# One output projection for both units of the sample, and layer 1's gates, transform and outputs in natural token order

## The chip, the core and the metric

The kernel runs on one core of a Trainium2 chip. The metric is the time of one execution in microseconds on the device. The kernel before took 1991.91 us (median of three runs: 1982.99, 1991.91, 1994.77).

## What is computed

A trunk of two layers is applied with the same weights to two groups of tokens: a prompt of 512 and a sample of 1024, 1024 channels wide, in float32. The change touches the second layer, called layer 1 in the code. Cut to what matters:

```python
def odd_layer(x, c, pre_g, post_g, ada_w, ada_b, w_in, w_out, rpb, lin):
    shift, scale, gate = adaln(c, ada_w, ada_b)
    h = rmsnorm(x, pre_g) * (1 + scale[:, None, :]) + shift[:, None, :]
    p = jnp.einsum('bsd,de->bse', h, w_in)
    qc, kc, vc, gc, ud, gd = split_cols(p, CD_SPLITS)      # 768, 768, 768, 768, 256, 256 columns
    oc = neighbourhood_attention(heads(qc), heads(kc), heads(vc), rpb).reshape(b, s, C_WIDTH)
    od = fourier_mixing(ud, lin)                           # real part of a 2-D DFT, then a linear map
    mixed = jnp.concatenate([oc * jax.nn.silu(gc), od * jax.nn.silu(gd)], axis=-1)
    y = rmsnorm(jnp.einsum('bse,ed->bsd', mixed, w_out), post_g)
    return x + gate[:, None, :] * y
```

The attention looks at a grid 64 tokens wide; a query sees a window of 8 rows by 16 columns.

## The kernel before

Tokens are worked on in units of 512: the sample's units 0 and 1, and the prompt as unit 2. Every matrix product is made of three products of rounded parts (high by high, high by low, low by high), so each operand exists twice, as `hh` and `hl`, and each weight as `who` and `wlo`: a weight block of 256 KB is loaded into a staging buffer `wso` (four of them), ScalarE casts the high part, and VectorE or GpSimd subtracts it to get the low part (`load_w`, L350). The pairs of high and low parts lie in rings: four pairs of tag `w`, and in layer 1 two more of tag `wx` (`w_pair`, L342).

Layer 1's attention works on blocks of queries, 8 grid rows by 16 columns. So its results are written in that order: within 512 tokens first the column block i, then the row r, then the column j. Before, all that meets the attention's result is in that order too: the gates (`chan_gemm` with `blocks`, L381, reads its tokens rearranged for q, g and d), the transform's result (by the order of the rows of its table, L79), and the rows of the residual input and of the outputs, which `blocks_of` (L267) picks out of DRAM as 8 groups of 16 rows.

The output projection `s3` (L845) is called for units 2, 0 and 1 in turn. For a unit it takes the operand, which `s3_operand` (L826) makes of eight pairs of loads, attention result `m` and gate `g` (name `og`): one multiply on GpSimd or VectorE, a cast on ScalarE and a subtraction on VectorE for each. Then come the gate row (`gate_row`, L254, 512 KB, one buffer), and four weight jobs of 256 columns: four weight blocks, two products groups of 48 matmuls each (`tok_gemm`, L366; two tiles of 128 tokens share one PSUM buffer, of which there are three), the squares on ScalarE (L863) and the product with the gate row on VectorE (L864). When a unit is through, the four residual rows `xo` of 512 KB are loaded into the three buffers of tag `sp`, in which the operand's loads lie too, the sum is made (L886) and the output row goes out. The next unit's operand is loaded under the former one's sums. So each unit loads all of `w_out_cd`, 4 MB, for itself.

All loads and stores are issued from SP's one queue in program order, and an issue that has to wait holds those behind it. A scheduler sets the order on each engine when the program is built.

## Time and profile before

| | us |
|---|---|
| three runs: lowest, median, highest | 1982.99, 1991.91, 1994.77 |
| profiled execution, its own time | 1982.05 |
| its span, first to last instruction | 1980.3 |
| TensorE busy in the span | 1895.3 (96%) |
| VectorE, ScalarE, GpSimd busy | 1219.5, 933.1, 636.3 |
| mean granted TensorE clock | 0.983 |

Busy times are of one profiled execution. In rows of the trace PE is TensorE, DVE VectorE, ACT ScalarE, POOL GpSimd and SPq the queue from which transfers are issued. L142 is line 142 of the kernel, out<-in are the program's names without buffer numbers, xN counts equal instructions, and a bracket at a row's end is the idle time before it and what ended that.

### The profile page before, as it was taken

The numbers are of one execution on the slowest core, as the hardware profiler recorded it, in microseconds if no ns is written. First come the engines' busy times: TensorE is split into PE (matmuls) and PEld (weight loads), VectorE is DVE, ScalarE is ACT, GpSimd is POOL, SyncE is SP. The second block draws the span as 40 slices with busy tenths as digits, with TensorE's granted clock in tenths as the row PEclk, the third lists the DMA queues.
The fourth block names the chain that finished last, engine by engine and source line by source line (L and its number), as shares of the span: only waits on it lengthen the run. The fifth ranks groups of instructions, "written<-read, shape, count | busy, mean of one in ns | idle before, by whom it ended". The sixth has DMA issues, their size and how long they took to land.

```text
span 1980.3 us, 38139 instructions
## 1 busy us (share of the span) xinstructions
PE 1895.3 (96%) x13720; PEld 1634.3 (83%) x13720; DVE 1219.5 (62%) x3139; ACT 933.1 (47%) x2211; POOL 636.3 (32%) x566
## 2 busy tenths in 40 slices
PE   6999999999999999999999999999999999998896
PEld 3889778999889888888876678888878888877895
DVE  3788765255768666767755686563766526667452
ACT  3466544343366544565544454454544424445331
POOL 2822334254622211121111222444323313344231
PEclk8999999999999999999999999999999999999998
DMA  9755555467764323344454775564777646687573
GB/s 339 226 175 170 165 177 176 143 204 226 249 222 129 110 76 95 99 143 132 134 159 153 225 231 172 190 205 141 231 215 230 188 141 191 191 245 232 183 228 105
DMA packets 270797, 358.75 MB, mean 181 GB/s; under 512 B 26648, under 2 KB 177528, under 8 KB 270608
## 3 DMA queue, kind: packets, MB, share of 16 engines
q1 hardware_dynamic: 270608, 356.32, 57.3%
q8 instruction: 108, 1.77, 0.4%
q14 instruction: 81, 0.66, 0.1%
HBM read 268.08 MB, written 88.16 MB: 180 GB/s over the span
## 4 chain that ended last, share of the span: by engine, by line
PE 77%; DMA 11%; DVE 6%; issue 2%; POOL 2%; ACT 1%; SPq 1%; ACTq 0%; DVEq 0%; POOLq 0%
PE y L142 7%; PE c1g L142 5%; PE c1q L142 5%; PE c1k L142 5%; PE t1v L142 5%; PE tvb L142 4%; PE gga L142 3%; PE ggb L142 3%; PE sas L142 3%; PE oas L142 3%; PE ptas L146 3%; PE tqa L142 2%; PE tqb L142 2%; DMA wso<-w_out_cd 2%; PE ocs L636 2%; PE sbs L772 2%
## 5 line engine op out<-in xcount | busy, mean ns | idle before, releaser
L142 PE MATMUL y<-who,hhm 128*128 128x256 f32 x768 | 220.6, 289 | 9.7 <-ACT hhm L841 4.9
L142 PE MATMUL y<-wlo,hhm 128*128 128x256 f32 x768 | 219.6, 288 | 7.5 <-POOL wlo L361 7.0
L142 PE MATMUL y<-who,hlm 128*128 128x256 f32 x768 | 218.8, 288 | 4.4 <-DVE hlm L842 4.3
L142 PEld LDWEIGHTS y<-who,hhm 128*128 128x128 f32 x768 | 147.9, 193 | 13.7 <-ACT hhm L841 5.6
L142 PEld LDWEIGHTS y<-wlo,hhm 128*128 128x128 f32 x768 | 147.9, 193 | 9.0 <-POOL wlo L361 7.4
L142 PEld LDWEIGHTS y<-who,hlm 128*128 128x128 f32 x768 | 148.4, 194 | 7.7 <-DVE hlm L842 5.3
L683 ACT ACTIVATE eas<-sas,nmas 128x512 f32<-128x512 f32 x128 | 86.8, 683 | 71.0 <-DVE nmas L679 70.9
L361 POOL TENSOR_TENSOR wlo<-wso,who 128x512 fp32r<-128x512 f32 x48 | 66.1, 1378 | 128.5 <-ACT who L360 119.2
L993 POOL TENSOR_TENSOR bics<-TTcs,mkc 128x288 f32<-128x288 f32 (+1 forms) x72 | 65.4, 910 | 127.7 <-DVE mcs L1006 106.5
L620 DVE TENSOR_TENSOR ptlas<-ptas,pthas 128x512 fp32r<-128x512 f32 x128 | 85.6, 684 | 18.6 <-ACT pthas L618 18.3
L674 DVE TENSOR_REDUCE mxas<-sas 128x1 f32<-128x512 f32 x128 | 86.4, 683 | 11.5 <-PE sas L142 10.7
L360 ACT CAST who<-wso 128x512 fp32r<-128x512 f32 x96 | 58.5, 616 | 63.3 <-DMA wso<-w_out_cd 22.6
L864 DVE TENSOR_TENSOR y<-y,rowg 128x256 f32<-128x256 f32 x96 | 39.9, 420 | 77.5 <-ACT ysq L863 66.7
L618 ACT CAST pthas<-ptas 128x512 fp32r<-128x512 f32 x128 | 70.3, 591 | 32.4 <-PE ptas L146 26.8
L142 PE MATMUL t1v<-wh1v,hl 128*128 128x256 f32 x288 | 82.5, 287 | 0.0
L142 PE MATMUL t1v<-wh1v,hh 128*128 128x256 f32 x288 | 82.0, 285 | 0.0
L142 PE MATMUL t1v<-wl1v,hh 128*128 128x256 f32 x288 | 81.6, 283 | 0.0
L1011 ACT ACTIVATE ecs<-ecs,ngmcs 128x288 f32<-128x288 f32 (+1 forms) x96 | 54.7, 571 | 54.6 <-DVE ngmcs L1009 53.2
L146 PE MATMUL ptas<-ident,eas 128*128 128x128 f32 x512 | 77.1, 272 | 1.5 <-DVE ptlas L620 1.5
L142 PE MATMUL oas<-ptlas,Vas 128*128 128x256 f32 x256 | 69.4, 297 | 1.1 <-DVE ptlas L620 1.1
L142 PE MATMUL oas<-pthas,Vas 128*128 128x256 f32 x256 | 69.1, 285 | 0.0
L863 ACT ACTIVATE ysq<-y 128x256 f32<-128x256 f32 x96 | 36.6, 382 | 67.9 <-PE y L142 49.9
(614 smaller groups left out, 6471.8 us busy)
## 6 DMA issues: line engine op xcount, KB each, us to landing
aw<-ada_w SPq DMA_DIRECT2D x48, 512.0 KB
wso<-w_out_ab SPq DMA_DIRECT2D x48, 256.0 KB
wso<-w_out_cd SPq DMA_DIRECT2D x48, 256.0 KB
kcs<-k1s SPq DMA_DIRECT2D x24, 384.0 KB
kbs<-k0s SPq DMA_DIRECT2D x16, 512.0 KB
ws1k<-w_in_cd SPq DMA_DIRECT2D x28, 256.0 KB
wskb<-w_in_ab SPq DMA_DIRECT2D x24, 256.0 KB
wsqb<-w_in_ab SPq DMA_DIRECT2D x24, 256.0 KB
```

What stands on the lines that cost most here:

```text
L142: self.nc.tensor.matmul(out, l, r, start=start, stop=stop, skip_group_check=True)
L146: self.nc.tensor.transpose(out, in_, self.ident[:k, :k])
L360: nc.scalar.copy(hi, st)
L361: (nc.vector if c in dve else nc.gpsimd).tensor_sub(lo, st, hi)
L618: nc.scalar.copy(h[:rows, :w], pt[:rows, :w])
L620: nc.vector.tensor_sub(lo[:rows, :w], pt[:rows, :w], h[:rows, :w])
L636: self.nc.tensor.matmul(out[x:x + HD], v, p, start=n < 2, stop=False, tile_position=(0, x), skip_group_check=True)
L674: nc.vector.tensor_reduce(mx[:, c:c + 1], ps, op=ALU.max, axis=AX.X, negate=True)
L683: nc.scalar.activation(e[:, 512 * c:512 * c + 512], pss[c], AF.Exp, bias=nmx, accum_out=den[:, c:c + 1])
L864: nc.vector.tensor_mul(ys[j][:, c], ps[:, t], G[:, c])
L993: nc.gpsimd.tensor_add(b, T[:, :, wo:wo + w], self.mcol[:, kind, wo:wo + w].unsqueeze(1).to_broadcast([P, nrow, w]))
L1011: nc.scalar.activation(e, e, AF.Exp, bias=ngm, scale=0.125, accum_out=den)
```

## The change

The sample's two units share their weights: a new `s3_two` takes the weight jobs in two halves, jobs 0 and 1 for unit 0 and then for unit 1, then jobs 2 and 3 for unit 0 and unit 1. The prompt still has an `s3` of its own, ahead of them. The gate row of the sample is loaded once, into the attention's one key buffer (tag `k`). In that stage weight pairs rotate through a ring of twelve (`self.wend`): four `w`, two `wx`, and buffers that the attention no longer needs (two of tag `q`, two of `pt`, two pairs out of `V`). Unit 0's sums lie in buffers of tag `e`, unit 1's in those of tag `x`.

Only the queries and the attention's result keep the block order. Gates, transform and the rows of residual and output are in the tokens' natural order; `s3_operand` reads the attention's result (k below 6) rearranged when it multiplies it by the gate, and writes the product over the gate.

```diff
@@ -75,8 +75,7 @@
         H, Q = S // 2, S // 4
         ang = lambda t, k: 2 * np.pi * ((t[:, None] * k[None, :]) % S) / S
         norm = 0.5 / np.sqrt(S * 64.0)
-
-        b = np.arange(S).reshape(S // 512, 8, 4, 16).transpose(0, 2, 1, 3).reshape(-1)
+        b = np.arange(S)
         t, quarter = np.arange(Q), np.array([Q])
         rows = []
         for k in (b[0::2], b[1::2]):
@@ -129,7 +128,7 @@
         self.gs, self.gp = self.G
         self.unit_of = [(self.gs, 0), (self.gs, 1), (self.gp, 0)]
 
-        self.wn, self.np, self.wx, self.rope_of = 0, 0, None, None
+        self.wn, self.np, self.wx, self.wend, self.rope_of = 0, 0, None, None, None
         self.pre, self.early, self.idle = {}, {}, True
 
 
@@ -251,8 +250,8 @@
             nc.vector.scalar_tensor_tensor(mod, mod, 1.0, self.adb[:, l, 2, ks].unsqueeze(2).to_broadcast([P, 4, 2]),
                                            op0=ALU.add, op1=ALU.mult)
 
-    def gate_row(self, l, g, nm):
-        t = self.sb.tile([P, D], F32, tag="row", name="row" + nm, bufs=RB)
+    def gate_row(self, l, g, nm, tag="row", bufs=RB):
+        t = self.sb.tile([P, D], F32, tag=tag, name="row" + nm, bufs=bufs)
         self.dma(t, self.modd[l][g.idx:g.idx + 1, :].to_broadcast([P, D]))
         return t
 
@@ -263,11 +262,6 @@
             src = self.a["x_sample" if g.idx else "x_prompt"][0][512 * (i // 4):512 * (i // 4) + 512]
             return src.rearrange("(a r) d -> r a d", r=4)[i % 4]
         return self.x1[g.name, i // 4][(i % 4) * P:(i % 4) * P + P, :]
-
-    def blocks_of(self, full, g, i):
-
-        v = full.rearrange("(h r i j) d -> h i r j d", r=8, i=4, j=16)
-        return v[i // 4, i % 4]
 
     def operand(self, nm, c):
         return (self.sb.tile([P, 2, 512], F32R, tag="hh", name=f"hh{nm}{c}", bufs=HB),
@@ -341,11 +335,14 @@
 
     def w_pair(self, shape, name):
         self.wn += 1
-        if self.wx and self.wn % (WB + WX) >= WB:
-            pool, tag, bufs = self.wx, "wx", WX
+        if self.wend:
+            tags, bufs = self.wend[self.wn % len(self.wend)]
+            pool = self.wx if tags[0][:2] == "wx" else self.sb
+        elif self.wx and self.wn % (WB + WX) >= WB:
+            pool, tags, bufs = self.wx, ("wxh", "wxl"), WX
         else:
-            pool, tag, bufs = self.sb, "w", WB
-        return [pool.tile(shape, F32R, tag=tag + x, name=f"w{x}{name}", bufs=bufs) for x in "hl"]
+            pool, tags, bufs = self.sb, ("wh", "wl"), WB
+        return [pool.tile(shape, F32R, tag=t, name=f"w{x}{name}", bufs=bufs) for x, t in zip("hl", tags)]
 
     def load_w(self, src, name, dve=()):
 
@@ -836,59 +833,103 @@
             st = pool.tile([P, 2, 512], F32, tag="sp", name=f"og{l}{u}{k}", bufs=SPB)
             self.dma(st[:, 0], self.md[l, n, k][:, us])
             self.dma(st[:, 1], self.gd[l, n, gu, k])
-            t = st[:, 0]
-            (nc.vector if k % 2 else nc.gpsimd).tensor_mul(t, t, st[:, 1])
+            t, m = st[:, 1], st[:, 0]
+            tv, mv = t, m
+            if l == 1 and k < 6:
+
+                tv, mv = t.rearrange("p (r i j) -> p r i j", r=8, i=4), m.rearrange("p (i r j) -> p r i j", r=8, i=4)
+            (nc.vector if k % 2 else nc.gpsimd).tensor_mul(tv, mv, tv)
             nc.scalar.copy(hh, t)
             nc.vector.tensor_sub(hl, t, hh)
         return [[o[i] for o in ops] for i in range(2)]
 
-    def s3(self, l, u, tag="x", H=None, step=None, last=None):
+    def s3_tiles(self, l, u, tag):
+
+        pool = self.sb
+        return ([pool.tile([P, D], F32, tag=tag, name=f"y{l}{u}{j}", bufs=XB if tag == "x" else EB) for j in range(4)],
+                [pool.tile([P, 4], F32, tag="yss", name=f"yss{l}{u}{j}", bufs=8) for j in range(4)])
+
+    def s3_w(self, l, u, job):
+        return self.load_w(self.a["w_out_ab" if l == 0 else "w_out_cd"][0][:, 256 * job:256 * job + 256], f"o{l}{u}{job}", W3)
+
+    def s3_job(self, l, u, H, G, w, job, ys, ss, after=None):
+
+        nc, pool = self.nc, self.sb
+        c = slice(256 * job, 256 * job + 256)
+        for jp in range(2):
+            ps = self.pD(f"y{l}{u}{job}{jp}").rearrange("p (t c) -> p t c", t=2)
+            self.tok_gemm(ps, H, w, jp)
+            for t in range(2):
+                j = 2 * jp + t
+                sq = pool.tile([P, 512], F32, tag="scr", name=f"ysq{l}{u}{job}{j}", bufs=SCB)
+                nc.scalar.activation(sq[:, 0:256], ps[:, t], AF.Square, accum_out=ss[j][:, job:job + 1])
+                nc.vector.tensor_mul(ys[j][:, c], ps[:, t], G[:, c])
+            if after:
+                after(jp)
+
+    def s3_x(self, l, u, j, tag):
+        g, gu = self.unit_of[u]
+        x = self.sb.tile([P, D], F32, tag=tag, name=f"xo{l}{u}{j}", bufs=SPB if tag == "sp" else XB)
+        self.dma(x, self.x_src(l, g, 4 * gu + j))
+        return x
+
+    def s3_end(self, l, u, jp, ys, ss, xs):
 
         nc, pool = self.nc, self.sb
         g, gu = self.unit_of[u]
         n = g.name
+        rs = []
+        for j in (2 * jp, 2 * jp + 1):
+            nm = f"{l}{u}{j}"
+            s1 = pool.tile([P, 1], F32, tag="ys1", name="ys1" + nm, bufs=2)
+            nc.vector.tensor_reduce(s1, ss[j], op=ALU.add, axis=AX.X)
+            rs.append(self.rsqrt(pool, s1, 1.0 / D, 1, "yr" + nm))
+        for t, x in enumerate(xs):
+            j = 2 * jp + t
+            y = ys[j]
+            nc.vector.scalar_tensor_tensor(y, y, rs[t], x, op0=ALU.mult, op1=ALU.add)
+            if l == 0:
+                self.dma(self.x1[n, gu].rearrange("(a r) d -> r a d", r=4)[j], y)
+            else:
+                i = 4 * gu + j
+                self.dma(self.o["y_sample" if g.idx else "y_prompt"][0][i * P:(i + 1) * P, :], y)
+
+    def s3(self, l, u, tag="x", H=None, step=None, last=None):
+
+        g = self.unit_of[u][0]
         H = H or self.s3_operand(l, u)
         G = self.gate_row(l, g, f"g{l}{u}")
-        ys = [pool.tile([P, D], F32, tag=tag, name=f"y{l}{u}{j}", bufs=XB if tag == "x" else EB) for j in range(4)]
-        ss = [pool.tile([P, 4], F32, tag="yss", name=f"yss{l}{u}{j}", bufs=4) for j in range(4)]
+        ys, ss = self.s3_tiles(l, u, tag)
         for job in range(4):
-            c = slice(256 * job, 256 * job + 256)
-            w = self.load_w(self.a["w_out_ab" if l == 0 else "w_out_cd"][0][:, c], f"o{l}{u}{job}", W3)
-            for jp in range(2):
-                ps = self.pD(f"y{l}{u}{job}{jp}").rearrange("p (t c) -> p t c", t=2)
-                self.tok_gemm(ps, H, w, jp)
-                for t in range(2):
-                    j = 2 * jp + t
-                    sq = pool.tile([P, 512], F32, tag="scr", name=f"ysq{l}{u}{job}{j}", bufs=SCB)
-                    nc.scalar.activation(sq[:, 0:256], ps[:, t], AF.Square, accum_out=ss[j][:, job:job + 1])
-                    nc.vector.tensor_mul(ys[j][:, c], ps[:, t], G[:, c])
+            self.s3_job(l, u, H, G, self.s3_w(l, u, job), job, ys, ss)
             if step:
                 step()
         r = last and last()
...
+        xt = "sp" if (l, u) in XSP else "x"
+        for jp in range(2):
+            self.s3_end(l, u, jp, ys, ss, [self.s3_x(l, u, j, xt) for j in (2 * jp, 2 * jp + 1)])
         return ys, r
+
+    def s3_two(self, l, H):
+
+        G = self.gate_row(l, self.gs, f"g{l}s", "k", KB)
+        Hs, Y = [H, None], [self.s3_tiles(l, 0, "e"), None]
+        for half in range(2):
+            ws = {}
+            for u in range(2):
+                if u == 1 and half == 0:
+                    Hs[1], Y[1] = self.s3_operand(l, 1), self.s3_tiles(l, 1, "x")
+                xs = {}
+                for job in (2 * half, 2 * half + 1):
+                    if u == 0:
+                        ws[job] = self.s3_w(l, 0, job)
+                    if job == 3:
+                        xs = {jp: [self.s3_x(l, u, j, "sp") for j in (2 * jp, 2 * jp + 1)] for jp in range(1)}
+
+                    def after(jp):
+                        x = xs.get(jp) or [self.s3_x(l, u, j, "sp") for j in (2 * jp, 2 * jp + 1)]
+                        self.s3_end(l, u, jp, *Y[u], x)
+                    self.s3_job(l, u, Hs[u], G, ws[job], job, *Y[u], after if job == 3 else None)
 
 
     def scratch1(self):
@@ -930,7 +971,7 @@
             return
         for c in range(2):
             ps = self.pD(f"c{nm}{c}")
-            self.chan_gemm(ps, H, w, c, typ in "qgd")
+            self.chan_gemm(ps, H, w, c, typ == "q")
             if typ == "q":
                 self.spill_hl(ps, self.qd[1, n, 2 * q + c], gu, 1.0, f"{nm}{c}")
             elif typ == "k":
@@ -1249,9 +1290,10 @@
                     if kind == "v2":
                         for q in range(3):
                             self.attn_c(gs, 1, q)
-            H = ops[0]
-            for u in (2, 0, 1):
-                _, H = self.s3(1, u, H=H, last=(lambda: self.s3_operand(1, (u + 1) % 3)) if u != 1 else None)
+            _, H = self.s3(1, 2, H=ops[0], last=lambda: self.s3_operand(1, 0))
+            self.wend = ([(("wh", "wl"), WB)] * WB + [(("wxh", "wxl"), WX)] * WX + [(("qh", "ql"), QB)] * QB +
+                         [(("pth", "ptl"), PTB)] * PTB + [(("V", "V"), VB)] * (VB // 2))
+            self.s3_two(1, H)
 
 
 @with_exitstack
```

The scheduler moves instructions in three places. The first is SP's queue where the sample's projection begins; `wso` is a weight block, `og` an operand's two halves (`m1s`, `g1s`), `rowg` the gate row, `y_prompt` an output row. Before:

```order
L139 DMA y_prompt<-y_23440 8x16x1024
L139 DMA wso_24357<-w_out_cd 128x2x256
L139 DMA og_24627<-m1s_126 128x512
L139 DMA og_24627<-g1s_118 128x512
L139 DMA rowg_24079<-mod_235 128x1024
L139 DMA wso_24363<-w_out_cd 128x2x256
L139 DMA y_prompt<-y_23441 8x16x1024
L139 DMA og_24633<-m1s_127 128x512
L139 DMA og_24633<-g1s_119 128x512
L139 DMA y_prompt<-y_23442 8x16x1024
L139 DMA og_24641<-m1s_128 128x512
L139 DMA og_24641<-g1s_120 128x512
```

and with the change:

```order
L138 DMA y_prompt<-y_23440 128x1024
L138 DMA og_24359<-m1s_126 128x512
L138 DMA og_24359<-g1s_118 128x512
L138 DMA wso_24787<-w_out_cd 128x2x256
L138 DMA wso_24793<-w_out_cd 128x2x256
L138 DMA y_prompt<-y_23441 128x1024
L138 DMA og_24365<-m1s_127 128x512
L138 DMA og_24365<-g1s_119 128x512
L138 DMA y_prompt<-y_23442 128x1024
L138 DMA og_24373<-m1s_128 128x512
L138 DMA og_24373<-g1s_120 128x512
L138 DMA og_24379<-m1s_129 128x512
```

Before, the operand of unit 1 begins there with the gate row, a weight and the prompt's outputs among its loads, and further weights behind; with the change its loads stand together behind the second prompt output, with the last two weights of the fourth job and two outputs among them.

The second place is ahead of it in the same queue, where the attention's last heads still run (`Vcs` are their values, `wso_23861` a weight of the prompt's last job). With the change:

```order
L138 DMA Vcs_22607<-v1s_196 128x1x384
L138 DMA og_24027<-m1s_132 128x512
L138 DMA Vcs_22609<-v1s_196 96x1x384
L138 DMA og_24027<-g1s_116 128x512
L138 DMA rowg1s<-mod_235 128x1024
L138 DMA og_24033<-m1s_133 128x512
L138 DMA wso_23861<-w_out_cd 128x2x256
L138 DMA og_24033<-g1s_117 128x512
```

The gate row of the sample (`rowg1s`) is new there; before, the operand's load `og_24033` followed `og_24027` at once.

The third is ScalarE's order at the attention's last two heads (`ofcs`, `ptccs` and `ecs` are the attention's; `who` a weight's cast, `ysq` a square of the projection's sums). Before:

```order
L630 COPY ptccs_22746<-ptcs_22742 96x384
L1011 ACTIVATE ecs_22795,dencs_22803<-ecs_22795,ngmcs_22801 128x288
L645 COPY ofcs_22708<-ocs_22619 64x512
L630 COPY ptccs_22790<-ptcs_22786 128x384
L863 ACTIVATE ysq_23788,yss_23443<-y_23739 128x256
L863 ACTIVATE ysq_23791,yss_23444<-y_23739 128x256
```

and with the change:

```order
L627 COPY ptccs_22746<-ptcs_22742 96x384
L1052 ACTIVATE ecs_22795,dencs_22803<-ecs_22795,ngmcs_22801 128x288
L357 CAST who_24097<-wso_24095 128x512
L642 COPY ofcs_22708<-ocs_22619 64x512
L627 COPY ptccs_22790<-ptcs_22786 128x384
L865 ACTIVATE ysq_23788,yss_23443<-y_23739 128x256
L357 CAST who_24103<-wso_24101 128x512
L865 ACTIVATE ysq_23791,yss_23444<-y_23739 128x256
```

Casts of the sample's first weights (`who_24097`, `who_24103`) have moved ahead of the attention's copy and of the square.

## Rows read from the trace of the kernel before

**Rows 1.** Windows by stage: length, busy time of each engine, clock, DMA share, GB/s.
```profile
core 0: us, PE busy (x) PEld busy (x) DVE busy (x) ACT busy (x) POOL busy (x), PEclk, DMA share, GB/s
1700.00:1760.00 60.00, 60.00 (x369) 48.31 (x369) 36.97 (x116) 24.96 (x62) 19.65 (x21) 1.00 0.64 199
1856.50:1963.20 106.70, 94.87 (x768) 94.06 (x766) 49.24 (x83) 34.26 (x99) 30.41 (x26) 0.95 0.59 193
1963.20:1980.30 17.10, 0.21 (x2) 0.01 (x1) 3.67 (x8) 0.95 (x4) 1.10 (x2) 0.64 0.44 147
```

**Rows 2.** Timeline of TensorE, 1856.5 to 1963.2 us: the products after a stop.
```profile
1875.39 0.58 PE L142 MATMUL y<-wlo,hhm 128*128 128x256 f32 x1 [6.06 <-POOL wlo L361]
...
1930.21 0.51 PE L142 MATMUL y<-who,hhm 128*128 128x256 f32 x1 [3.28 <-DVE y L864]
...
1940.60 0.38 PE L142 MATMUL y<-who,hhm 128*128 128x256 f32 x1 [1.52 <-ACT who L360]
...
1941.94 0.39 PE L142 MATMUL y<-wlo,hhm 128*128 128x256 f32 x1 [0.96 <-POOL wlo L361]
```

**Rows 3.** Windows behind the long stop and in the stage's undisturbed end.
```profile
1875.40:1877.40 2.00, 2.00 (x9) 2.00 (x10) 1.99 (x4) 1.61 (x7) 1.61 (x1) 0.50 0.86 295
...
1946.00:1963.20 17.20, 17.20 (x147) 17.20 (x146) 6.06 (x13) 4.08 (x14) 2.39 (x3) 1.00 0.03 7
```

**Rows 4.** Timeline of VectorE: products with the gate row that waited for it.
```profile
1874.02 0.42 DVE L864 TENSOR_TENSOR y<-y,rowg 128x256 f32<-128x256 f32 x1 [4.93 <-DMA rowg<-mod]
...
1928.70 0.42 DVE L864 TENSOR_TENSOR y<-y,rowg 128x256 f32<-128x256 f32 x1 [5.75 <-DMA rowg<-mod]
```

**Rows 5.** Groups of instructions, 1856.5 to 1963.2 us: casts of weights.
```profile
L360 ACT CAST who<-wso 128x512 fp32r<-128x512 f32 x27 | 16.4, 616 | 23.7 <-DMA wso<-w_out_cd 22.6 <-PE y L142 0.8
```

**Rows 6.** Tile og: issues and low parts, unit 1 in layer 1, then layer 0.
```profile
L139 SPq DMA_DIRECT2D og<-m1s x8: 319/339/793, 1861.2 to 1892.9; - x8
...
L842 DVE TENSOR_TENSOR hlm<-og,hhm x8: 680/694/1777, 1874.8 to 1899.2; 128x512 fp32r<-128x512 f32 x8
...
L139 SPq DMA_DIRECT2D og<-m0p x8: 319/380/467, 317.3 to 338.5; - x8
...
L842 DVE TENSOR_TENSOR hlm<-og,hhm x8: 684/693/1781, 324.7 to 345.7; 128x512 fp32r<-128x512 f32 x8
```

**Rows 7.** The end: chain of waits (one row), then timeline of VectorE.
```profile
1961.67 10.07 DMA xo<-x_s
...
1965.39 1.28 DVE L886 SCALAR_TENSOR_TENSOR y<-y,yr112r,xo 128x1024 f32<-128x1024 f32 x1
...
1971.84 1.28 DVE L886 SCALAR_TENSOR_TENSOR y<-y,yr113r,xo 128x1024 f32<-128x1024 f32 x1 [5.11 <-DMA xo<-x_s]
```

**Rows 8.** Windows: loads near the start, and residual and output rows alone.
```profile
20.00:40.00 20.00, 16.35 (x106) 9.79 (x104) 6.76 (x7) 5.93 (x10) 8.32 (x6) 0.94 1.03 360
...
1968.00:1973.00 5.00, 0.00 (x0) 0.00 (x0) 1.16 (x1) 0.00 (x0) 0.00 (x0) 0.50 0.51 207
```

**Rows 9.** Windows of the key products (first) and of the query products alone.
```profile
1266.00:1700.00 434.00, 71.50 (x288) 52.74 (x288) 8.25 (x12) 6.93 (x12) 1.00 0.62 191
...
1266.00:1700.00 434.00, 72.91 (x288) 53.02 (x288) 8.25 (x12) 7.04 (x12) 1.00 0.62 191
```

**Rows 10.** Timelines of TensorE, SP and ScalarE at the last heads; a page group.
```profile
1813.76 0.30 PE L142 MATMUL scs<-kcs,qlcs 128*128 128x288 f32 x1
...
1815.36 0.76 SPq L139 DMA_DIRECT2D og<-g1s  x1
...
1828.05 2.95 SPq L139 DMA_DIRECT2D wso<-w_out_cd  x2
...
1834.97 0.58 ACT L645 COPY ofcs<-ocs 64x512 f32<-64x512 f32 x1 [1.35 <-PE ocs L636]
...
L993 POOL TENSOR_TENSOR bics<-TTcs,mkc 128x288 f32<-128x288 f32 (+1 forms) x72 | 65.4, 910 | 127.7 <-DVE mcs L1006 106.5
```

23 lines of the change are left out of this document (removed).

## Prediction

> **What bounds the kernel now.** I read the windows by stage first. While layer 1's gates are projected TensorE is busy for 60.00 of 60 us; from the sample's first output product to its last (1856.5 to 1963.2 us, 768 products) it is busy for 94.87 of 106.70; behind the last product 17.10 us pass in which it does nothing [rows 1]. So the early part is bound by TensorE, and the last 124 us are where a change of loads and order can pay. Next I looked for TensorE's stops in that stage: four, 6.06, 3.28, 1.52 and 0.96 us, 11.8 together, which is all that is missing from the busy time [rows 2]. Then the clock: undisturbed it starts 147 products in 17.2 us at a granted 1.00, one every 0.117 us; just after the long stop 9 in 2 us at 0.50, 1.2 GHz, one every 0.21 [rows 3]. 768 products at 0.117 are 89.9 us, so 106.7 - 89.9 = 16.8 us is the most this stage can give: 11.8 of stops, 5.0 of restarts at the low clock.
>
> What ends the stops? VectorE's product with the gate row waits 4.93 and 5.75 us for the row's load, at 1874.02 and 1928.70 [rows 4]; it is what empties the three PSUM buffers, and TensorE starts again at 1875.39 and 1930.21. There is one buffer for that row, and its load can only be issued when the former unit is through with it. The last two stops name ScalarE's cast and GpSimd's low part of a weight [rows 2]; of the casts, 27 in the stage, 22.6 us of idle time before them ends with a weight's landing [rows 5]. The second unit loads the same 4 MB again.
>
> **What the change takes and adds, stage by stage.**
>
> *The sample's projection.* Sixteen weight loads of 256 KB, 16 casts of 0.62 us and 16 low parts go. The gate row is loaded once, into the attention's key buffer, some 45 us before it is used, so neither wait of [rows 4] is left. Twelve pairs of buffers (four ordinary, two of layer 1, six of the attention) let three of the four weight jobs be made while the prompt's sums still run. All four stops lose their cause. What is late next is unit 1's operand: it was needed after four jobs of unit 0, now after two. Two jobs are 192 products, 22.5 us, so it is wanted at 1856.5 + 22.5 = 1879. Its first load stands behind the second prompt output in SP's queue, as before (1861.2), so I start it at 1860. Bounds for its length: in layer 0, with fewer weights between its loads, a stream of eight took from the first issue at 317.3 to the end of the last low part at 346.4 (345.7 and a median 0.69), 29.1 us; in this stage it took from 1861.2 to 1899.9, 38.7 us, with nine weight loads, the gate row and two prompt outputs among its loads [rows 6]. Now two weight loads and two outputs stand among them (the SP rows in the section on the change), so I take the 29: done at 1889. TensorE's new order spends the wait on the other pair of token tiles; behind its last wait 45 products of the first job are left, 5.3 us. So that job ends at 1894.3 instead of 1879 + 96 x 0.117 = 1890.2: 4 us late. Between nothing and 13.7 (1899.9 - 1.2 + 5.3 - 1890.2) I keep 4.3, stop and restart together. Gain 16.8 - 4.3 = **12.5**, bounds 1 and 16.8.
>
> The operand's multiply now reads its attention half in runs of 16 elements. No row of before has this on 512 elements; GpSimd's addition of a mask over rearranged rows takes 910 ns for 288 [rows 10], 3.2 ns an element, so 1.6 us at that rate, and nothing extra is the other end. It lies inside the stream's three buffers and inside the bounds above; I add nothing. Without that cover three GpSimd products of a unit would cost 5 us.
>
> *The end.* The fourth residual row is issued at 1961.67 and lands 10.07 us later; VectorE could have used it when the third's sum was through (1965.39 + 1.28, and a root behind it: about 1967.4), and begins at 1971.84: 4.4 us late. From its end (1973.1) to the end of the span the last output takes 7.2 us [rows 7, 1]. In that stretch nothing but such rows moves, at 207 GB/s with a DMA share of 0.51; loads over 128 partitions near the start move 360 GB/s at 1.03 [rows 8]. Rows in natural order are such 128-partition transfers. If they run like those, the fourth row has landed by 1967 and costs nothing; and the last output's 512 KB take 1.5 us instead of 2.5. I take 4.4 + 1.0 = **5.4**; the bounds are 0 (half the engines still) and 7, where what is left of the third output is out of the way too.
>
> The Trainium skill has a rule on this (DMA: Bandwidth & Descriptors, section "Why a DMA increments its semaphore by 16 and not by 1"): a transfer is spread over the largest number of engines, up to 16, that divides the slowest dimension on both of its sides. By it a row written as 8x16x1024 has 8 engines and one written as 128x1024 has 16; the trace agrees for the first (share 0.51), no row of this stage shows the second. By the rule the term is the 5.4, by the low bound 0.
>
> *Gates and transform in natural order.* Gate and transform-gate products read contiguous tokens, as keys did. Keys: 288 products in 71.50 us; queries, which keep the rearranged read: 72.91, 4.9 ns more for each [rows 9]. 576 gate products change, 2.8 us at most. Part is given back to loads that bound the stretch behind; **1.5**, bounds 0 and 2.8. The table of the transform changes its values, not its size.
>
> *What it costs earlier.* The gate row waits in SP's queue for the last use of the key buffer. SP came to that place at about 1816 (the issue ahead is at 1815.36), and TensorE's last product with that key is over at 1814.06 [rows 10]: no wait, but 512 KB go ahead of the next operand's and a weight's load. On ScalarE a weight's cast now stands ahead of the attention's copy of the last-but-one head, which began at 1834.97; the weight's load was issued in the two that began at 1828.05 and take 2.95 to issue [rows 10], so about 1830.5. If it lands in 4 to 5 us the copy is 0.5 to 1 us late; behind the copy TensorE waits for the last head. If it takes the 8 to 10 us of a loaded queue, 4 to 6. I take **1** lost, bounds 0 and 6.
>
> *Sum:* 12.5 + 5.4 + 1.5 - 1 = 18.4 us off the profiled execution's 1982.05 (span 1980.3 and 1.75 around it): 1963.6. The three timed runs lie higher, mean 1989.9, 7.8 above the profiled one; I put the same on top: **1971 us**.
>
> **Rivals.**
> - *No stop left:* operand in time, 16.5 + 6.5 + 2.8 - 0 = 25.8, 1964. For it: half the operand's competitors are gone and rows move faster. Chance 0.17.
> - *Operand as late as before:* 38.7 us again, since its three buffers are still shared with the residual rows and two outputs leave meanwhile. 1 + 5.4 + 1.5 - 1 = 6.9, 1983. Chance 0.14.
> - *Natural order moves no faster:* the share of 0.51 has another cause, and the change of form does nothing. 12.5 + 0 + 1.5 - 1 = 13, 1977. Against it [rows 8]. Chance 0.12.
> - *Casts ahead of attention:* 6 lost instead of 1, 1976. Chance 0.11.
> - *Slower:* the gate row's wait for the key buffer holds SP's queue, in which operand, weights and residual rows stand behind. Each us of it is one us. It turns the sum round from 18.4 on, that is if the buffer came free after 1834.4; were it held until 1844.4, 10 us beyond that, the time would be 1971 + 28.4 = 1999. Against it: 1814.06. Chance 0.03.
>
> **How the numbers follow.** The forecast has 0.43. Leaving out most of the slow side and the tip of the fast one gives 1958 to 1985, which also takes in whether the runs fall as the profiled one or 8 above. A change of 1% (1972 here, from the median 1991.91) is about what a measurement can tell. Below it lie the first rival, a good half of the forecast and a little of the others: 0.45. Slower by over 1% needs 40 us lost: 0.03. Within 1%: 0.52.
>
> **What will show it.** No VectorE wait on a gate row behind 1850; seven of the eight jobs without a stop; one group of stops in unit 1's first job, ended by operand casts, of 0 to 5 us together; DMA share near 1 while rows alone move; at the end under 12 us behind the last product. Wrong if stops appear around 1830 to 1840, if unit 1's first job stops over 8 us, if the last rows still show a share of 0.5, or if weights of the fourth job come late.

## The result: about 30 us faster, at the forecast range's lower end, and not by the shared weights

| | before | after |
|---|---|---|
| timed runs beside each other, median (lowest to highest), us | 1989.6 (1982.99 to 1994.77) | 1957.32 (1955.01 to 1960.37) |
| a second set, us | 1988.42 (1982.14 to 1996.22) | 1959.49 (1957.62 to 1961.44) |
| ratio, first and second set | | 0.985 (0.9825 to 0.9875), 0.9852 (0.9832 to 0.9872) |
| profiled execution and its span, us | 1982.05, 1980.3 | 1960.37, 1958.6 |

The forecast was 1971 us in a range of 1958 to 1985; the first median lies 0.7 us below that range and the second 1.5 above its lower end, 13.7 and 11.5 us under the forecast. The medians differ by 32.3 us in the first set and by 28.9 in the second; the ratio is a gain of 1.2 to 1.8%.

**Where the time went.** Windows of the kernel after, columns as in [rows 1]: the sample's projection, what lies behind its last product, and a stretch in which rows of residual and output alone move.

```profile
1858.10:1949.50 91.40, 90.96 (x770) 90.56 (x768) 37.89 (x72) 22.56 (x77) 14.25 (x15) 1.00 0.44 151
1949.50:1958.60 9.10, 0.01 (x1) 0.00 (x0) 3.72 (x8) 0.95 (x4) 1.10 (x2) 0.72 0.58 230
...
1930.00:1935.00 5.00, 5.00 (x45) 5.00 (x44) 2.35 (x5) 1.00 (x4) 0.55 (x1) 1.00 0.98 360
```

The stage fell from 106.7 to 91.4 us, with TensorE busy in all but 0.44, and what lies behind it from 17.1 to 9.1 [rows 1]. Together that is 23.3 us. Rows that had moved at a share of 0.51 and 207 GB/s move at 0.98 and 360 [rows 8]. Of the four stops of [rows 2] none is left, and the granted clock of the stage is 1.00, where it was 0.95. The one stop of that stage is a new one, in unit 1's first job (timeline of TensorE, after):

```profile
1884.04 0.39 PE L141 MATMUL y<-who,hlm 128*128 128x256 f32 x1 [0.44 <-DVE hlm L843]
```

VectorE waits for no gate row there, so [rows 4] have no successor. Unit 1's operand, which took 38.7 us from its first issue to its end [rows 6], takes 25.7 (1860.74 to 1886.46; tile og, first issues and the last low part's group):

```profile
L138 SPq DMA_DIRECT2D og<-m1s x8: 319/342/827, 1860.7 to 1880.0; - x8
...
L843 DVE TENSOR_TENSOR hlm<-og,hhm x8: 677/692/1795, 1869.0 to 1885.8; 128x512 fp32r<-128x512 f32 x8
```

The end, to be laid beside [rows 7] (timelines of SP's queue and of VectorE, after): the fourth residual is issued at 1947.57, and the fourth sum no longer waits for it but for its own root (`yr`, of the norm).

```profile
1947.57 0.43 SPq L138 DMA_DIRECT2D xo<-x_s  x1
...
1951.52 1.29 DVE L890 SCALAR_TENSOR_TENSOR y<-y,yr112r,xo 128x1024 f32<-128x1024 f32 x1
...
1953.60 1.29 DVE L890 SCALAR_TENSOR_TENSOR y<-y,yr113r,xo 128x1024 f32<-128x1024 f32 x1 [0.73 <-POOL yr113r L153]
```

All of this is what the prediction said would be seen. The experiments show that the main reason was nevertheless another than the one it gave.

### The profile page after: what moved, and what is told of

Read it like the earlier page. It is cut to its first block, busy times and chain, and to the rows that moved or that the text cites. A ratio compares the mean times of both kernels' runs of the same rounds, so it can differ in the third digit from the quotient of the medians.

```text
span 1958.6 us, 38066 instructions
## 1 busy us (share of the span) xinstructions
PE 1892.0 (97%) x13720; PEld 1630.5 (83%) x13720; DVE 1207.7 (62%) x3131; ACT 925.5 (47%) x2195; POOL 625.8 (32%) x558
## 4 chain that ended last, share of the span: by engine, by line
PE 78%; DMA 9%; DVE 7%; issue 2%; POOL 2%; ACT 1%; SPq 1%; POOLq 0%; ACTq 0%; DVEq 0%
PE y L141 9%; PE c1q L141 5%; PE c1g L141 5%; PE c1k L141 5%; PE t1v L141 5%; PE tvb L141 4%; PE ggb L141 3%; PE gga L141 3%; PE sas L141 3%; PE oas L141 3%; PE ptas L145 3%; PE tqb L141 2%; PE tkb L141 2%; PE tqa L141 2%; PE tkva L141 2%
## 5 line engine op out<-in xcount | busy, mean ns | idle before, releaser
L671 DVE TENSOR_REDUCE mxas<-sas 128x1 f32<-128x512 f32 x128 | 86.4, 683 | 11.6 <-PE sas L141 10.8
L358 POOL TENSOR_TENSOR wlo<-wso,who 128x512 fp32r<-128x512 f32 x40 | 54.3, 1360 | 98.6 <-ACT who L357 91.7
L615 ACT CAST pthas<-ptas 128x512 fp32r<-128x512 f32 x128 | 70.4, 591 | 32.1 <-PE ptas L145 26.6
L357 ACT CAST who<-wso 128x512 fp32r<-128x512 f32 x80 | 48.8, 616 | 42.2 <-issue 15.4
L842 ACT CAST hhm<-og 128x512 fp32r<-128x512 f32 x48 | 29.7, 619 | 79.7 <-POOL og L841 44.1
```

Of the source, the lines that this page charges most:

```text
L357: nc.scalar.copy(hi, st)
L358: (nc.vector if c in dve else nc.gpsimd).tensor_sub(lo, st, hi)
L615: nc.scalar.copy(h[:rows, :w], pt[:rows, :w])
L671: nc.vector.tensor_reduce(mx[:, c:c + 1], ps, op=ALU.max, axis=AX.X, negate=True)
L842: nc.scalar.copy(hh, t)
```

## Experiments

Times are medians beside runs of the kernel before on the same chip, with the ratio to those and its 95% interval. "Stage" is from the first to the last of the sample's 768 products, which for the first profile of before is 107.15 us by the rows of TensorE's timeline; "tail" is the rest of the span (16.88 there; 91.41 and 9.09 in the kernel after). Both are of one profiled execution of each kernel. A row of residual or output is called narrow below in the form 8x16x1024 and wide in the form 128x1024. Diffs are cut to the lines that matter.

### 1. The changed kernel and the kernel before once more

No edit in either.

> The changed kernel once more, for a second profile. In the first one layer 1's keys began 3.0 us later than before (832.9 against 829.9), and the stage of the sample's projection 1.8 us later (1858.3 against 1856.5). Theory: that is scatter between executions of code that the change does not touch; here the keys begin anywhere from 828 to 833, the stage takes 91 us again (90 to 92.5), the tail behind the last product 9.1 (8.5 to 9.7), and the time is 1953 to 1961. Rival: the change costs the early part about 3 us, so the keys begin within 0.5 us of 832.9 again.

Measured: 1959.49 us, ratio 0.9852 (0.9832 to 0.9872). Keys began at 829.9, as in the first profile of before; stage 91.6, tail 9.1. So the 3 us of late start in the first profile of after was scatter, and the change costs nothing ahead of layer 1.

> The kernel before once more, for a second profile. In the first the sample's stage began 1026.4 us after layer 1's first key product, in the three kernels with residual rows in 8x16 form that were profiled since (shared weights in block order, one gate row, natural outputs) 1031.4 to 1032.0, in those with natural or 16x8 rows 1025.1 to 1027.2. Theory: the 8x16 residual rows of the prompt also cost about 5 us ahead of that stage in most executions, and the first profile of before caught one in which they did not; here the distance is 1029 to 1033 and the time above 1985. Rival: the distance is 1026 again, and the 5 us belong to the edits of those kernels.

Measured: 1986.61 us, one execution, with stage 108.0 and tail 16.9. From the first key product to the stage it took 1027.6 us, so the theory (1029 to 1033) fell and the rival (1026) came nearer, by one more profile. What makes the other kernels reach the stage later is taken up under "Open" below. By these second profiles the two spans differ by 1984.8 - 1955.8 = 29 us, by the first by 21.7. The first profiled execution of before was quicker than each of its timed runs (1982.05 against 1982.99 and more), and that of after was as slow as the slowest of its four.

### 2. One part at a time

**Sharing alone**: of the changed kernel, the natural order is taken out.

```diff
-        b = np.arange(S)
+        b = np.arange(S).reshape(S // 512, 8, 4, 16).transpose(0, 2, 1, 3).reshape(-1)
-            self.chan_gemm(ps, H, w, c, typ == "q")
+            self.chan_gemm(ps, H, w, c, typ in "qgd")
-            (nc.vector if k % 2 else nc.gpsimd).tensor_mul(tv, mv, tv)
+            (nc.vector if k % 2 else nc.gpsimd).tensor_mul(t, t, st[:, 1])
-        self.dma(x, self.x_src(l, g, 4 * gu + j))
+        self.dma(x, self.blocks_of(self.x1[g.name, gu], g, j) if l else self.x_src(l, g, 4 * gu + j))
-                self.dma(self.o[...][0][i * P:(i + 1) * P, :], y)
+                self.dma(self.blocks_of(self.o[...][0], g, i), y)
```

> The changed kernel with the block order kept for gates, transform, residual and output rows: only the sharing of weights, the single gate row and the ring of buffers are left of the change. Theory (as the prediction has it: the shared weights and the early gate row empty the stage of stops, the natural order gives the end): stage 91 to 95 us instead of 106.7, tail behind the last product 14 to 17 us, gate products 402 to 404 ns in the mean as before; time 1966 to 1972. By the prediction's own sum (12.5 less 1) it would be 1978. Rival: the natural order carries a good part of the stage too, since the prompt's outputs in 8x16 form hold up unit 1's operand; then unit 1's first job stops for 4 us or more, the stage takes 97 or more, and the time is 1975 to 1980.

Measured: 1983.38 us, ratio 0.9965 (0.995 to 0.9981). The rival held for the stage and the stops, and the time is 3 us above its range: stage 99.7, tail 17.8, and five stops of 5.2 us together from 23 to 32 us into the stage, four of them (4.7 us) named by unit 1's operand.

**Natural order alone**: of the kernel before, the same five places are changed the other way; every unit still loads its own weights and gate row. TensorE's products come in the same order as in the kernel before.

> The kernel before with the natural order alone: gates, transform, residual and output rows; each unit still loads its own weights and gate row. Theory: the stage keeps its four stops and takes 104 to 108 us; the tail shrinks from 17.1 to 9 to 11 us, the gate products gain about 2 us; time 1979 to 1984, 6 to 10 below before. Rival 1: faster rows also shorten the stops, since gate row and weights share the queues with the rows; stage 98 to 101, time 1972 to 1976. Rival 2: the tail was shorter in the changed kernel because of its own order (the residual rows issued earlier), not of the form of the rows; tail 14 or more, time within 3 us of before.

Measured: 1958.49 us, ratio 0.9843 (0.9818 to 0.9868), the whole of the change's gain. Windows of this kernel, the stage and what lies behind it:

```profile
1858.60:1949.70 91.10, 91.08 (x769) 90.88 (x768) 48.52 (x83) 34.72 (x99) 31.63 (x26) 1.00 0.67 226
1949.70:1958.70 9.00, 0.00 (x0) 0.00 (x0) 3.67 (x8) 0.95 (x4) 1.10 (x2) 0.69 0.60 231
```

No stop at all, although the sample's weights are loaded, cast and split twice, as before. Rival 1 had the direction, but not the size; my own theory, that the stage keeps its four stops, fell.

**One gate row**: of the kernel before, only this (`gate_row` takes the tag and the number of buffers, as in the change).

```diff
-        G = self.gate_row(l, g, f"g{l}{u}")
+        if l and u < 2:
+            if u == 0:
+                self.Gs = self.gate_row(l, g, f"g{l}s", "k", KB)
+            G = self.Gs
+        else:
+            G = self.gate_row(l, g, f"g{l}{u}")
```

> The kernel before with one edit: the sample's gate row is loaded once, into the attention's key buffer, and serves both units; every unit still loads its own weights. Theory: VectorE's waits of 4.93 and 5.75 us for the row are gone, and with them TensorE's stops of 6.06 and 3.28 and their restarts at the low clock; stage 95 to 98 instead of 106.7, time 1979 to 1982. Rival: the weights' landing is what is late next, the casts waited 22.6 us for it; the stops come back in another place, named by casts and low parts, stage 103 or more, time 1985 to 1990.

Measured: 1989.13 us, ratio 1.0008 (0.9991 to 1.0024). Nothing is gained, as the rival had it; the stage is 109.9 us in the profiled execution, which at 1996.26 was the slowest of ten. The waits for the row are gone, and two long stops are still there, 20 and 84 us into the stage (19 and 74 before; timeline of TensorE), now both named by weights:

```profile
1887.30 0.58 PE L142 MATMUL y<-wlo,hhm 128*128 128x256 f32 x1 [5.62 <-POOL wlo L361]
...
1952.12 0.58 PE L142 MATMUL y<-who,hhm 128*128 128x256 f32 x1 [5.25 <-ACT who L360]
```

So the gate row's single buffer was not what bound that stage. Row and weights were late together, and taking the row's wait away left the weights'.

### 3. What in the natural order does it

**Rows alone**: of the kernel before, the 24 residual and output rows of layer 1 in natural order.

```diff
-                self.dma(x, self.blocks_of(self.x1[n, gu], g, j))
+                self.dma(x, self.x_src(l, g, i))
-                    self.dma(self.blocks_of(self.o[...][0], g, 4 * gu + j), y)
+                    self.dma(self.o[...][0][(4 * gu + j) * P:(4 * gu + j + 1) * P, :], y)
```

> The kernel before with one edit: the residual and output rows of layer 1 are transferred in natural order, 128x1024 instead of 8x16x1024. Gates, transform and operand stay in block order, so the rows are added and written to the wrong tokens; the work is the same. Theory A (new, after the natural order alone gave 30 us): the rows in 8x16 form are the cause of the stops, since each keeps half the transfer engines busy twice as long and every weight, gate row and operand behind it in those engines lands later; then the time is 1959 to 1963, the sample's stage 91 us and the tail 9. Theory B: the gates' and the operand's order carry the gain, by TensorE's products and the path of the operand; then the stage keeps its stops and only the tail shrinks, 1978 to 1984.

Measured: 1960.57 us, ratio 0.987 (0.9841 to 0.99); stage 91.1 without a stop, tail 9.0. Theory A held. How the rows had held up the rest is seen in the chain of waits of the kernel before (start, us from issue to landing):

```profile
1854.03 8.49 DMA y_prompt<-y
1862.91 11.09 DMA rowg<-mod
1875.37 7.28 DMA wso<-w_out_cd
...
1924.19 15.64 DMA wso<-w_out_cd
```

A gate row of 512 KB takes 11.09 us to land, issued behind two output rows and a residual row; the weights of 256 KB in that chain take 7.28 to 15.64. With the 24 rows wide VectorE's two waits for the gate row (4.93 and 5.75 us) are one of 1.56, though the row is still loaded once for each unit into its one buffer (timeline of VectorE, rows alone):

```profile
1915.88 0.42 DVE L864 TENSOR_TENSOR y<-y,rowg 128x256 f32<-128x256 f32 x1 [1.56 <-DMA rowg<-mod]
```

**Another form in pieces, 16x8x1024**: one edit in `blocks_of` of the kernel before.

```diff
-        v = full.rearrange("(h r i j) d -> h i r j d", r=8, i=4, j=16)
+        v = full.rearrange("(h r i j) d -> h i r j d", r=16, i=4, j=8)
```

> The kernel before with the rows of residual and output taken as 16x8x1024 instead of 8x16x1024: 128 rows that are still not contiguous, but with 16 as the slowest dimension. They are other rows than those wanted, so the result is of other tokens; bytes and packets are the same. Theory A1: what counts is that only 8 engines share a transfer whose slowest dimension is 8; with 16 the stops go as with natural rows: 1959 to 1964, DMA share near 1 where rows move alone. Theory A2: it is the broken form, by longer issues (0.63 us rather than 0.36 for a row, 24 rows) or scattered addresses; then it stays at 1983 to 1990 with a share near 0.5.

Measured: 1962.58 us, ratio 0.9883 (0.9854 to 0.9912); stage 92.2 with one stop of 0.74, tail 10.8. Theory A1 held: the rows are still scattered in pieces, and a row still takes 591 ns to issue (641 in the 8x16 form, 356 in natural order, medians of the eight sample outputs), yet 23.9 of the 25.9 us of rows alone are there. Windows of this kernel, behind its last product: over these 3 us, in which rows move alone, the share is 0.96.

```profile
1952.00:1955.00 3.00, 0.00 (x0) 0.00 (x0) 1.51 (x3) 0.00 (x0) 0.55 (x1) 0.50 0.96 307
```

**Four engines, 4x32x1024**: the same line, with r=4 and j=32.

> The kernel before with the rows of residual and output taken as 4x32x1024, so that the slowest dimension is 4 (other rows than those wanted; bytes, packets and instructions the same). Theory A1 (a transfer has as many engines as its slowest dimension allows): a row keeps 4 engines busy, four times as long as over 16; the share where rows move alone falls from 0.5 to about 0.25 and the rate from 207 to about 104 GB/s; what 8 engines cost against 16 in excess (24 us of 1986 against 1962) is paid with three times the excess length for a row instead of one, so 2010 to 2050, most likely near 2035, with a tail of 25 us or more. Theory A2 (broken forms are all alike below 16): 1983 to 1992 and a share of 0.5.

Measured: 2036.04 us, ratio 1.0253 (1.0237 to 1.027); stage 144.7, tail 29.2, as theory A1 had it. Windows of this kernel, behind its last product, and its group of weight casts in the stage, with the idle time before them and what ended it:

```profile
2016.00:2026.00 10.00, 0.00 (x0) 0.00 (x0) 0.04 (x1) 0.00 (x0) 0.00 (x0) 0.50 0.25 105
```

```profile
L360 ACT CAST who<-wso 128x512 fp32r<-128x512 f32 x27 | 16.4, 616 | 51.3 <-DMA wso<-w_out_cd 50.2 <-PE y L142 0.8
```

Share and rate are half those of the 8x16 form, and about a quarter of the wide one's: 0.25, 0.51 and 0.98, and 105, 207 and 360 GB/s. The Trainium skill says that such a transfer is spread over the largest number of engines, at most 16, that divides the slowest dimension on both of its sides (DMA: Bandwidth & Descriptors, section "Why a DMA increments its semaphore by 16 and not by 1"). The shares here agree: a slowest dimension of 4 gave 0.25, one of 8 gave 0.51, and 16 and 128 gave 0.96 and 0.98. The casts' wait for weights is 50.2 us in this kernel, 22.6 in the kernel before [rows 5], and in the kernel with rows alone there is none in the stage's group:

```profile
L360 ACT CAST who<-wso 128x512 fp32r<-128x512 f32 x27 | 16.5, 617 | 8.2 <-PE y L142 6.4 <-issue 1.9
```

**Residual or output rows alone**: one of the two edits of rows alone each.

> The kernel before with only the residual rows' loads in natural order, the output rows' writes as before (the sums are of wrong tokens). Theory A: twelve of the 24 rows leave the slow form, so about half of the 30 us is gained: 1971 to 1978, of it 4 in the tail, where the last residual was late; the stop of the first unit, behind the prompt's outputs, stays, and the second unit's shrinks. Rival: writes are what holds the engines, loads are harmless; then only the tail's 4 us go, 1983 to 1987.

> The kernel before with only the output rows' writes in natural order, the residual rows' loads as before (the rows written are of wrong tokens). Theory A: the other half: 1971 to 1978; the stop of 6 us in the first unit goes, since four prompt outputs stood ahead of the gate row and the weights there, and some of the second unit's stays. Rival: loads are what counts; then only 2 to 3 us in the tail go, 1984 to 1988.

Measured: residual alone 1975.24 us, ratio 0.9945 (0.9927 to 0.9963), stage 98.3, tail 16.2; outputs alone 1969.5 us, ratio 0.992 (0.9895 to 0.9946), stage 99.4, tail 10.4 (profiled in the slowest of six executions, 1977.31). Both loads and writes count; the two gains, 11.2 and 16.9 us, add up to 28.1, and both together gave 25.9. Theory A has the size for the residual rows, is 1.5 us too slow for the outputs, and has most of the places: with natural residuals unit 0 still stops for 3.75 us and unit 1 for 0.96, with natural outputs unit 0 for 1.25 and unit 1 for 2.66 and 0.97. The tail went otherwise than I expected: natural outputs shorten it by 6.5 us, natural residuals by 0.7.

### 4. What the rest of the change is worth

**8x16 rows in the changed kernel**: its two row edits as in "sharing alone", the rest natural.

> The changed kernel with one edit: its residual and output rows in 8x16x1024 form again (rows of wrong tokens); gates, transform and operand stay in natural order. Theory A: the rows' form is nearly all of the change's gain, so 1978 to 1983; against the kernel that shares weights with everything in block order (1983.4) the gates' natural order is worth the 3 us that their products became shorter (405 to 399 ns, 576 of them) or less; stage 97 to 100, tail 16 to 18, stops of 3 to 6 us in unit 1's first job, for the operand. Rival: the sharing needs the natural gates and operand to work, then 1962 to 1970.

Measured: 1981.01 us, ratio 0.9978 (0.996 to 0.9996); stage 100.2, tail 17.2. Theory A held. Two of its stops (timeline of TensorE):

```profile
1884.78 0.58 PE L141 MATMUL y<-who,hhm 128*128 128x256 f32 x1 [2.43 <-ACT hhm L847]
...
1890.48 0.58 PE L141 MATMUL y<-who,hhm 128*128 128x256 f32 x1 [0.94 <-ACT hhm L847]
```

With one of 0.87 between them they are three in unit 1's first job, 4.2 us with the operand's casts and low parts named; another of 0.60 stands ahead of them. That is the size the prediction forecast for the changed kernel itself (4.3); there the rows were wide, and the operand came earlier.

**A later operand**: three loads ahead of unit 1's operand in the changed kernel.

```diff
                 if u == 1 and half == 0:
+                    for q in range(3):
+                        st = self.sb.tile([P, 2, 512], F32, tag="sp", name=f"extra{q}", bufs=SPB)
+                        self.dma(st.rearrange("p a b -> p (a b)"), self.x_src(l, self.gs, q))
                     Hs[1], Y[1] = self.s3_operand(l, 1), self.s3_tiles(l, 1, "x")
```

> The changed kernel with three loads of 512 KB, read by nothing, ahead of unit 1's operand in the same queue and buffers. The prediction took that operand for what is late next; in the changed kernel its stops were 0.44 and 0.67 us. Theory: it stands on the edge, so what delays it shows at once: three such loads are 4.4 us at 360 GB/s and up to 10 at the pace of the operand's own loads (25.7 us for eight), so stops of 4 to 10 us in unit 1's first job, time 1962 to 1969. Rival: there is slack, the loads run together with the prompt's outputs; stops under 2 us, time 1956 to 1961.

Measured: 1961.07 us, ratio 0.9883 (0.9866 to 0.99); stage 93.7, three stops of 2.24 together (timeline of TensorE):

```profile
1884.23 0.38 PE L141 MATMUL y<-who,hhm 128*128 128x256 f32 x1 [0.87 <-ACT hhm L842]
1886.18 0.50 PE L141 MATMUL y<-who,hlm 128*128 128x256 f32 x2 [0.98 <-DVE hlm L843]
```

This lies between theory and rival. The loads did delay the operand: its first load is issued 9.5 us into the stage instead of 2.6, and its last low part ends 35.4 us into it (1886.9 with a start at 1851.5), in the changed kernel 28.4 (1886.46, 1858.1). Of these 7 us only 1.8 became stops. Most of the rest lies in TensorE's order, which the scheduler made anew, and which differs from the 204th to the 311th product of the stage: when the last low part is through, 276 products have begun instead of 235. At 0.117 us each the 41 are 4.8 us.

So the operand is what is late next, and the order of products has slack for about 5 us of it.

## Why the prediction was near in time and wrong in its cause

**The stage's bound** was right: at most 16.8 us, from 768 products at 0.117. The stage gave 15.7 (107.15 to 91.41).

**The step that failed** is the first of the sample's projection: "it is what empties the three PSUM buffers" and "There is one buffer for that row", with "The second unit loads the same 4 MB again" for the rest. The waits were read rightly, their cause wrongly. I took a load that is late for one that is issued late or once too often, and did not ask how long it took from issue to landing. The trace had that: 11.09 us for the gate row, 7 to 16 for weights. With natural rows the same loads, as many as before, are in time; with one gate row alone nothing is gained; with sharing alone 7.5 us of the stage are. By the prediction's own terms sharing alone was to give 11.5 us (12.5 less 1) and the natural order 6.9 (5.4 and 1.5); they gave 5.0 and 29.9. That the time came near all the same was luck: both parts were in one change.

**The rule was applied in the wrong place.** The prediction knew that 8x16 rows keep half the engines, by the share of 0.51, and used it for the tail only, where rows move alone. The same form was issued 16 times from 1854.0 to 1923.5, four outputs and a residual of the prompt, four outputs and seven residuals of the sample, among weights, gate rows and operands. An estimate from the rates: 512 KB take 2.53 us at 207 GB/s and 1.46 at 360, so 16 rows are 17.2 us longer; the stage lost 16.0 (107.15 against the 91.13 of rows alone). At 105 GB/s a row takes 4.99, which makes 56.6; it lost 53.5 (144.66). With half the rows narrow it is 8.6, and 7.1 and 8.3 were lost. So in the kernel before nearly each microsecond that a row takes longer is one of TensorE's. In the changed kernel with 8x16 rows 8.8 are lost (100.24 against 91.41), and the stops name the operand and no weight.

By the Trainium skill an engine works through its descriptors in the order of its ring (DMA: Bandwidth & Descriptors, section "Queues, rings and completion order"). A wide load would then wait for its share on the engines that the narrow row keeps busy. The landing times agree, and so does a window of the kernel before in which the gate row is on its way from its issue at 1917.16 to 1928.70 [rows 4], with four narrow rows issued from 1919.91 to 1923.48:

```profile
1920.00:1925.00 5.00, 5.00 (x45) 5.00 (x44) 2.46 (x2) 1.86 (x3) 1.37 (x2) 1.00 0.53 203
```

A share of 0.53 is about eight engines and a half of 16, so the others stand idle while a wide load is awaited; with the rows alone made wide the share around that load is 1.01 (1907 to 1917). The profile doesn't tell one engine from another, so that the missing pieces wait on just the engines that the narrow rows keep busy is argued and not shown.

**Unit 1's operand late, 4.3 us**: mis-sized. It measured 0.44 and 0.67. I took 29 us for its length from a stream of layer 0; it took 25.7. With 8x16 rows left in place it took 33.0 (1862.4 to 1895.4), and the stops were 4.8 in all.

**The end, 5.4 us** with an upper bound of 7: it gave 7.8 (16.88 to 9.09), above the bound. The fourth residual's lateness, 4.4, was right: the fourth sum begins 4.1 us behind the last product where it began 8.4 behind it. But it was late mostly because narrow outputs were ahead of it: with natural residuals alone the last of them still lands 9.38 us after its issue and the sum begins 7.7 us behind the last product, with natural outputs alone 5.4. The mis-sized term is the last output, 1.0: from the end of the fourth sum to the end of the span 7.2 us became 3.7, so it measured 3.5. With natural outputs alone that piece is 3.8, with natural residuals alone 7.2. I had counted only what the one row saves by itself.

**Gates, 1.5 us**, bounds 0 and 2.8: read as the prediction read keys and queries, by the busy time of all products of a kind, 432 gate products fell from 111.10 to 108.99 us and 144 of the transform's gate from 36.91 to 36.17, together 2.85, which is the upper bound. One of the groups, before and after (busy us of the group, mean ns of one product):

```profile
L142 PE MATMUL c1g<-hh,wl1g 128*128 128x512 f32 x144 | 58.0, 404 | 0.0
```

```profile
L141 PE MATMUL c1g<-hh,wl1g 128*128 128x512 f32 x144 | 57.0, 397 | 0.0
```

In the times it does not show beyond the scatter: natural order alone is 2.1 us below rows alone, and 8x16 rows in the changed kernel 2.4 below sharing alone, but these pairs were timed beside different runs of the kernel before, and counted from those the differences are 4.1 and -0.2.

**What it costs earlier, 1 us**: from the first key product to the stage 1026.4 and 1027.6 us before, 1025.2 twice after, with the gates' gain in it. Right within the scatter of executions. The gate row's place in SP's queue cost nothing that shows.

**The offset of 7.8 us** for runs over the profile was not there for the kernel after: its runs lie between 5.4 us below its first profiled execution and 1.1 above it. The sum, 18.4, was 6 to 8 us too small: stage, tail and the stretch from the first key product give 15.7 + 7.8 + 1.2 = 24.7 in the first pair of profiles and 16.4 + 7.8 + 2.4 = 26.6 in the second. With the offset the first pair makes 14.1 us, close to the 13.7 by which the forecast lay above the first median.

**The rivals.** "No stop left" (1964) is what came, by a mechanism that no rival named. "Natural order moves no faster" is refuted by the rates of the four forms. "Casts ahead of attention" did not show in the changed kernel, where the cast began at 1834.84 without a wait and no stop lies at 1830 to 1840. But it did in the two kernels that share weights with narrow rows: there the cast waits for its weight, the attention's copy `ofcs` stands behind the cast, and TensorE behind the copy (timelines of ScalarE and TensorE, 8x16 rows in the changed kernel):

```profile
1835.89 0.62 ACT L362 CAST who<-wso 128x512 fp32r<-128x512 f32 x1 [6.55 <-DMA wso<-w_out_cd]
...
1838.00 2.39 PE L638 MATMUL ocs<-ptccs,Vcs 96*64 96x128 f32 x18 [4.27 <-DVE ofcs L648]
```

With sharing alone wait and stop are 4.94 and 2.66 us. So that rival's mechanism was real, and it was the wide rows that kept it out of the result.

**What would show it** came out as listed, and did not tell the causes apart: no gate row wait, few stops, a share near 1 and a short tail all follow from wide rows alone. What would have told them apart was the time from issue to landing of a weight.

**Open:** the timed medians differ by 32.3 and 28.9 us, of which the two pairs of profiles show 24.7 and 26.6; where the rest lies, in code that the change does not touch, is not settled. Nor is all of another difference: sharing alone and 8x16 rows in the changed kernel reach the stage 1031.4 and 1030.0 us after their first key product, 6.2 and 4.8 later than the kernel after, of which the stop at the attention's last head, 2.66 and 4.27, is a part. One gate row and outputs alone take 1032.0 and 1031.8, the kernel before 1026.4 and 1027.6, and the kernel with 4x32 rows, which has narrower rows still, 1025.5; why is open.

## What to carry to other kernels

Before a late load is taken for one too many or a buffer too few, read how long it takes from issue to landing, and what was issued ahead of it: here transfers over few engines made the wide ones behind them late, though the mean DMA share of the stage (0.59) showed room. Look at the slowest dimension of each transfer's form: 8x16x1024 against 128x1024, or against 16x8x1024 where rows must stay in pieces, was worth 25.9 and 23.9 us of the change's 30. And list signs that only one of the causes would leave, since a forecast time can hold for a wrong reason.

## What the runs showed that was not expected

- Rate and share of a 512 KB row go with the slowest dimension: 105 GB/s at 4, 207 at 8, 360 at 128; a scattered form with 16 had 307 GB/s and a share of 0.96, over 3 us.
- In the kernel before, the time that narrow rows take longer went into the stage nearly whole: 16 rows of 1.07 us more (from the rates) made it 16.0 us longer.
- A wait can move into work that the change does not touch: with narrow rows and shared weights a late weight held up the attention's copy, and TensorE stopped for 4.27 us ahead of the stage.
- Halving the sample's weight loads (DMA share of the stage 0.67 to 0.44) moved nothing once the rows were wide: 1958.49 us with all loads, 1957.32 and 1959.49 with half. With narrow rows it was worth 5.0 us, with the one gate row and the ring of buffers in it.
